# Two-layer recurrent decoder step: layer 1 planned with VectorE alone waiting for GpSimd; half-size products for the second head of layer 2, built from a copy of the normed x1 in DRAM

## The chip, the cores and the metric

The kernel runs on one core of one Trainium2 chip, as a single launch. The metric is the device time of that launch in microseconds (us); lower is better. The kernel before took 1070.28 us (median of three runs: 1069.11, 1070.28, 1070.42).

## The reference

1056 tokens (1024 of a prompt and 8 sequences of 4) with 1024 features go through two layers and a last norm, all in float32:

```python
def _lru_layer(x, ...):                 # layer 1 of the text (Hawk)
    u = _rmsnorm(x, g_norm) @ w_in      # 1024 -> 2 * 1536
    xb, gate = u[..., :W_LRU], u[..., W_LRU:]
    xc, new_buf = _causal_conv(xb, conv_w, conv_b, buf)
    h, h_last = _rg_lru(xc, w_r, b_r, w_i, b_i, lam, h0)
    return x + (h * silu(gate)) @ w_out, h_last, new_buf

def _hgrn_layer(x, ...):                # layer 2 of the text (HGRN2), 8 heads of 128
    u = _rmsnorm(x, g_norm) @ w_in      # 1024 -> 4 * 1024: q, f, v, gate
    log_g = logaddexp(log(lb), log1p(-lb) + log_sigmoid(f));  k = -expm1(log_g)
    o, S_T = _hgrn2_chunked(silu(q), k, v, log_g, S0)         # decayed linear attention, states 128 x 128
    return x + (rmsnorm(o) * o_gain * silu(gate)) @ w_out, S_T
...
y = _rmsnorm(x, final_gain)             # outputs: y of both groups of tokens, and all new states
```

## The kernel before

**Products.** Tokens lie along the free dimension, features on the 128 partitions. Every float32 product is three TensorE matmuls in a 32-bit format of shorter mantissa, summed in PSUM (`mm3`, L248, L249, L250): a rounded part `xh` or `whi` of either operand and the rest `xl` or `wlo`, as xh*whi + xl*whi + xh*wlo. The rounding is a ScalarE cast, the rest a subtraction on VectorE or GpSimd (`subtract`, L331, weights and activations alike).

**Chunks.** Layer 1 and the first part of layer 2 work on three chunks `c` of 352 tokens (`CH`). A product of 128 output features of layer 2 over all tokens is then 3 chunks x 8 blocks of input features x 3 = 72 matmuls of 352 columns.

**Heads of layer 2.** A head `h` needs four products: q, f, v and gate, items 0 to 3. Heads 0 and 1 (`HC = 2`) compute all items in full. From head 2 on, items go in pairs (0, 1) and (3, 2), and each pair is one two-by-two block product by Strassen and Winograd (`seven`): seven half-size products instead of eight, each over 264 tokens (`QT`) at a time, 2 x 4 x 3 = 24 matmuls of 264 columns. They need sums of weights (VectorE, L1441) and sums `t` of the normed x1, taken between the token halves (`HT` = 528 apart) and the feature halves. A string like "126b74b35" sets the order of the seven products, and `b` in it places a burst of the head's other work.

**The sums t.** `build` makes three of the four sets of sums, TB[2], TB[3] and TB[4], from `xh` and `xl` with seven VectorE operations of 264 columns for each of 8 pieces (j, x) (L1371), three casts on ScalarE (L1374), and three remainders on GpSimd (L331). `build1` makes the fourth set in place over the upper token half of the first four blocks of `xh` and `xl`, so only when the full products no longer read them: 8 pieces with three VectorE additions and one VectorE remainder each. Product 6 reads TB[2], products 7 and 4 TB[4] and TB[3], product 5 the fourth set.

**The bursts.** The recurrence of a head is four bursts of small work on all engines (`burst1` to `burst4`), placed between the large products; burst 4 ends with `turned(h)`: v and the weighted keys of head h go to DRAM (`vt`, `kt`) and come back with the token blocks on other partitions, each as one store of 512 KB and four loads of 128 KB. `states` (L1216, TensorE) of the next head's burst 2 reads both. The gated output of a head is stored to DRAM (`yd`, 528 KB) by `gated`.

**What sets the order.** Each layer's operations are recorded with an engine, an estimated duration, the buffers read and written, and a priority (`Flow.add`). `Flow.plan` is a list scheduler over all engines, repeated with the times of `back`; for layer 1 a random search of 3000 tries over the first 60 us follows. The order that comes out is issued as it stands, so every engine and the SP queue, which issues nearly all DMAs, work in a fixed order, and an instruction that waits holds up what stands behind it there. The planner has a model of VectorE and GpSimd getting in each other's way: a two-input VectorE operation that starts while GpSimd works is lengthened until GpSimd is done (`taken`), and a GpSimd operation that starts during such a VectorE operation is lengthened likewise (`locked`).

In the trace `sg`, `R`, `tmp`, `a` and `k` are large work buffers with changing contents, `hg` and `mm` PSUM banks, `t` the cast sums, `wraw` weights as loaded, and `si` the incoming states.

Of the kernel before, what the change touches and what calls it, by code (L numbers as in the profile page):

```python
# [42 lines left out]
NCH = 3  # L43
# [8 lines left out]
class Flow:  # L52
# [7 lines left out]

    def __init__(self, until=None, side=1.2, busy=None):


        self.until = until
        self.busy = {e: (busy or {}).get(e, 0.0) for e in self.ENGINES}
# [37 lines left out]
    def plan(self, key, stop=None):  # L103
# [11 lines left out]
        for _ in range(n):  # L115
# [101 lines left out]
def tile_trunk(ctx: ExitStack, tc: tile.TileContext, xT, prm, hc, w0, wg, wo0, w1, wo1, s_in,  # L217
# [18 lines left out]
    def pc(name, j, n=1):  # L236
        a = PRM[name][0] + j
        return P[:, a:a + n]
# [33 lines left out]

    x1a = [nc.dram_tensor(f"x1a_{m}", (128, TOK), F32, kind="Internal").ap() for m in range(KD)]
    x1d = [nc.dram_tensor(f"x1_{m}", (128, TOK), F32, kind="Internal").ap() for m in range(KD)]

# [27 lines left out]
    with ExitStack() as l0:  # L303
        pl = l0.enter_context(tc.tile_pool(name="l0", bufs=1, reuse_waits="tile"))
        fl = Flow("PE")

# [8 lines left out]

        def dma(dst, src, r=(), w=(), prio=5, kb=180, q=Q):
            fl.add("SP" if q is Q else "ACT", 0.45, lambda: q.dma_start(dst, src), r, w, prio, kb * (1.0 if r else 0.75))

# [337 lines left out]
        def out_last(src):  # L656
# [42 lines left out]
            for c in range(NCH):  # L699
# [233 lines left out]
    with ExitStack() as l1:  # L933
# [229 lines left out]
        def turned(h, row, rk, dst, key, keys):  # L1163

            d = turn[key, h % 2]
            dve(1024, lambda: V.transpose(dst, row[:, :1024].rearrange("p (n b i) -> p b n i", n=8, b=4)), rk, keys, 3, True)
            dma(d, dst, keys, ((key, "d", h % 2),), 3, 512)
            back = d.rearrange("(a i) (b m) -> b i a m", a=4, b=4)
            for b in range(4):
                dma(dst[32 * b:32 * b + 32].rearrange("p (a m) -> p a m", a=4), back[b], ((key, "d", h % 2),), (keys[b],), 3, 128)  # L1170

# [136 lines left out]
        def gated(h, s, sk):  # L1308
# [41 lines left out]
        def build(j, temps):  # L1350

            for x in range(2):
                t, tk = next(temps)
                lo, up = slice(x * QT, x * QT + QT), slice(HT + x * QT, HT + x * QT + QT)
                q, k = lo, ("x12", j, x)
                F = lambda o: o.bitcast(F32)
                chain = ((3, (xh[j + 4], up, 1), (xh[j], up, -1), (xl[j + 4], up, 1), (xl[j], up, -1)),
                         (2, (xh[j], lo, 1), (xl[j], lo, 1)), (4, (xh[j + 4], lo, 0), (xl[j + 4], lo, 1)))
                for n, *steps in chain:
                    if n == 3:  # L1360
                        (a, u, _), (b, v, _), *steps = steps
                        add(QT, t, F(a[:, u]), F(b[:, v]), ALU.subtract, (k,), tk)
                    for a, u, sign in steps:
                        if sign == 0:
                            add(QT, t, F(a[:, u]), t, ALU.subtract, (tk,), tk)
                        else:
                            add(QT, t, t, F(a[:, u]), ALU.add if sign > 0 else ALU.subtract, (tk, k), tk)
                    parted_sum(n, j, x, TB[n, 0][:, j, q], TB[n, 1][:, j, q], t, tk, G)

# [6 lines left out]

        def build1(temps):

            for j in range(4):
                for x in range(2):  # L1380
                    t, tk = next(temps)
                    lo, up = slice(x * QT, x * QT + QT), slice(HT + x * QT, HT + x * QT + QT)
                    F = lambda o: o.bitcast(F32)
                    h, l = xh[j], xl[j]
                    k = ("x12", j, x)
                    add(QT, t, F(h[:, up]), F(h[:, lo]), ALU.subtract, (k,), tk)
                    add(QT, t, t, F(l[:, up]), ALU.add, (tk, k), tk)
                    add(QT, t, t, F(l[:, lo]), ALU.subtract, (tk,), tk)
                    for i in range(2):
                        inherit(("T", 1, i, j, x), [k, *((("xh", "xl")[i], j, c) for c in (1, 2))])  # L1390
                    parted_sum(1, j, x, h[:, up], l[:, up], t, tk, V)

# [129 lines left out]
        own_gate(0)  # L1522
        spots = [(R[:, 3, i * QT:i * QT + QT], ("tmp", 2 + i)) for i in range(4)]
        small_ = [(tmp[:, i], ("tmp", i)) for i in range(2)]
        temps = cycle(small_ + spots)
        for j in range(4):
            build(j, temps)
        for h in range(HC):
            order = [item(h, i) for i in ((0, 1, 3, 2) if h else (3, 2))]
            seq_ = [(i, c) for i in range(len(order)) for c in range(NCH)]  # L1530
            if h == HC - 1:
                seq_ = seq_[:-6] + [(len(order) - 2 + i, c) for c in (2, 1, 0) for i in (0, 1)]
            ws2 = {} if h else ahead
            for n, (i, c) in enumerate(seq_):
# [3 lines left out]
                if h and n == 5:  # L1538
# [4 lines left out]
        build1(cycle(small_))  # L1543
        mm, hg = cycle(banks8[:NM7]), cycle(banks8[NM7:])
# [12 lines left out]

        for h in range(HC, H):
            seven(h, 0, 1, FQ0 if h == HC else FQ, (lambda h=h: burst3(h - 1), lambda h=h: burst4(h - 1)))
            own_gate(h)  # L1560
            seven(h, 3, 2, GV, (lambda h=h: burst1(h), lambda h=h: burst2(h)))

# [252 lines left out]
```

## Time and profile before

| | before |
|---|---|
| median of three runs | 1070.28 us |
| span of the profiled execution | 1069.7 us |
| TensorE matmuls | 1045.4 us busy, 98% |
| VectorE | 817.2 us, 76% |
| ScalarE | 574.2 us, 54% |
| GpSimd | 520.1 us, 49% |
| moved by DMA | 119.89 MB, 112 GB/s |

The profile counts an engine busy from the start of an instruction to its end. Matmuls overlap one another, so TensorE's 98% says that something is nearly always in flight; what one matmul takes is read from the distance between two starts. The profiled execution's own time is its span, with nothing of the program outside it; it lies 0.6 us under the median of the runs. Layer 1 ends near 510 us, where the first products of layer 2 take over. A clock of 1.00 means that TensorE's clock was granted in full.

### The profile page before, as it was taken

The page shows a single profiled execution, that of the slowest core. Times are in us where ns is not written, and L with a number is a line of the kernel's source. Part 1 is how long each engine was busy: PE and PEld are TensorE (multiplying, and loading weights), DVE is VectorE, ACT ScalarE, POOL GpSimd, SP SyncE. Part 2 cuts the span into 40 slices and gives each one's busy share as a digit, 9 for nine tenths or more (in the row PEclk, how much of TensorE's full clock was granted, in tenths as well). Part 3 has the DMA queues.
Part 4 walks back from the last instruction along what each step waited for, and adds up shares of the span by engine and source line. Part 5 has one row for each costly group of instructions (what it writes and reads, how often), then busy time and mean ns, then how long its engine had stood idle before and what let it go on. Part 6 is the DMA issues. An engine that isn't in the chain of part 4 may idle for free.

```text
span 1069.7 us, 26257 instructions
## 1 busy us (share of the span) xinstructions
PE 1045.4 (98%) x10220; PEld 1013.1 (95%) x10220; DVE 817.2 (76%) x1626; ACT 574.2 (54%) x1308; POOL 520.1 (49%) x601
## 2 busy tenths in 40 slices
PE   9899999999999999999999999999999999999997
PEld 9789999999999999999999998999999999999986
DVE  8999667589698788454697899787878787995436
ACT  6576745966856786433344363544545454562324
POOL 2425234345345355735567455555555554652544
PEclk9999999999999999999999999999999999999999
DMA  8201112212681387432113015242424242577204
GB/s 282 78 14 56 37 44 61 68 53 67 182 258 56 104 265 245 147 111 73 59 62 104 9 61 162 81 150 73 140 83 140 84 139 84 164 222 217 85 1 163
DMA packets 81644, 119.89 MB, mean 112 GB/s; under 512 B 10480, under 2 KB 59632, under 8 KB 81520
## 3 DMA queue, kind: packets, MB, share of 16 engines
q1 hardware_dynamic: 79216, 115.46, 34.4%
q10 hardware_dynamic: 2304, 2.77, 0.7%
q8 instruction: 80, 1.31, 0.5%
q14 instruction: 44, 0.36, 0.1%
HBM read 79.44 MB, written 33.87 MB: 106 GB/s over the span
## 4 chain that ended last, share of the span: by engine, by line
PE 85%; DVE 9%; issue 2%; DMA 1%; POOL 1%; ACT 0%; SPq 0%; ACTq 0%; POOLq 0%; DVEq 0%
PE mm L248 24%; PE mm L250 23%; PE mm L249 23%; PE hg L1216 2%; PE hg L1063 1%; PE hg L1271 1%; PE hg L575 1%; DVE sg L466 1%; PE hg L1273 1%; DVE xl L331 1%; PE hg L249 1%; PE hg L250 1%; PE hg L248 1%; DVE k L507 1%; DVE R L441 1%
## 5 line engine op out<-in xcount | busy, mean ns | idle before, releaser
L248 PE MATMUL mm<-xh,whi 128*128 128x352 f32 (+1 forms) x1143 | 358.6, 314 | 0.0
L250 PE MATMUL mm<-xh,wlo 128*128 128x352 f32 (+1 forms) x1143 | 354.8, 310 | 1.1 <-POOL wlo L331 1.1
L249 PE MATMUL mm<-xl,whi 128*128 128x352 f32 (+1 forms) x1143 | 354.3, 310 | 0.5 <-POOL xl L331 0.5
L331 POOL TENSOR_TENSOR wlo<-wraw,whi 128x256 fp32r<-128x256 f32 (+3 forms) x184 | 198.9, 1097 | 214.8 <-ACT whi L386 114.9
L249 PEld LDWEIGHTS mm<-xl,whi 128*128 128x128 f32 x1143 | 215.8, 189 | 2.2 <-POOL xl L331 0.8
L248 PEld LDWEIGHTS mm<-xh,whi 128*128 128x128 f32 x1143 | 215.5, 189 | 1.7
L250 PEld LDWEIGHTS mm<-xh,wlo 128*128 128x128 f32 x1143 | 215.6, 189 | 1.4 <-POOL wlo L331 1.4
L507 DVE SCALAR_TENSOR_TENSOR k<-xb,prm_sb,k 128x352 f32<-128x352 f32 (+2 forms) x144 | 87.0, 615 | 23.0 <-ACT k L504 19.9
L248 PE MATMUL mm<-t,whi 128*128 128x264 f32 (+1 forms) x306 | 89.6, 293 | 0.1
L249 PE MATMUL mm<-t,whi 128*128 128x264 f32 (+1 forms) x306 | 87.7, 287 | 0.0
L250 PE MATMUL mm<-t,wlo 128*128 128x264 f32 (+1 forms) x306 | 87.5, 286 | 0.0
L1504 DVE TENSOR_TENSOR k<-mm,k 128x264 f32<-128x264 f32 x144 | 60.1, 424 | 23.4 <-PE mm L250 21.7
L331 POOL TENSOR_TENSOR wlo<-R,whi 128x256 fp32r<-128x256 f32 x64 | 56.0, 895 | 28.1 <-ACT whi L1431 27.1
L590 POOL TENSOR_TENSOR k<-X 128x352 f32<-128x352 f32 x36 | 44.2, 1235 | 46.6 <-DVE R L591 32.7
L386 ACT CAST whi<-wraw 128x512 fp32r<-128x512 f32 (+2 forms) x83 | 46.3, 575 | 27.8 <-PE mm L249 12.4
L248 PEld LDWEIGHTS mm<-t,whi 128*128 128x128 f32 x306 | 57.5, 188 | 0.9 <-ACT krep L1003 0.3
L250 PEld LDWEIGHTS mm<-t,wlo 128*128 128x128 f32 x306 | 57.7, 189 | 0.0
L249 PEld LDWEIGHTS mm<-t,whi 128*128 128x128 f32 x306 | 57.6, 188 | 0.0
L1431 ACT CAST whi<-wraw 128x512 fp32r<-128x512 f32 x52 | 32.0, 618 | 41.6 <-PE mm L250 13.9
L248 PE MATMUL mm<-yh,whi 128*128 128x352 f32 x153 | 51.3, 336 | 0.0
L250 PE MATMUL mm<-yh,wlo 128*128 128x352 f32 x153 | 49.4, 323 | 0.0
L249 PE MATMUL mm<-yl,whi 128*128 128x352 f32 x153 | 49.4, 323 | 0.0
(459 smaller groups left out, 2557.9 us busy)
## 6 DMA issues: line engine op xcount, KB each, us to landing
wraw<-in_w_dram SPq DMA_DIRECT2D x90, 256.0 KB, 2.9
wraw<-in_wo_dram SPq DMA_DIRECT2D x34, 192.0 KB, 2.5
si<-in_s_in_dram SPq DMA_DIRECT2D x8, 512.0 KB, 5.5
vt<-sg SPq DMA_DIRECT2D x8, 512.0 KB, 2.9
sg<-vt SPq DMA_DIRECT2D x32, 128.0 KB, 3.0
kt<-kt SPq DMA_DIRECT2D x8, 512.0 KB, 3.0
kt<-kt SPq DMA_DIRECT2D x32, 128.0 KB, 4.3
out_ss_out_dram<-si SPq DMA_DIRECT2D x8, 512.0 KB, 2.7
```

The lines of the kernel that those rows point to most:

```text
L248: T.matmul(out, wh, xh, start=first, stop=False)
L249: T.matmul(out, wh, xl, start=False, stop=False)
L250: T.matmul(out, wl, xh, start=False, stop=last)
L331: emit = lambda: e.tensor_tensor(b, x, a.bitcast(F32), op=ALU.subtract)
L386: act(m, lambda hi=hi, raw=raw, m=m: S.copy(hi[:, :m], raw[:, :m]), rk, (hk,), prio)
L441: (pool if e is G else dve)(CH, lambda: e.tensor_tensor(a[:, :CH], a[:, :CH], sq, op=ALU.add), (sk, ak), (ak,), 2)
L466: dve(CH, lambda: V.scalar_tensor_tensor(x, x, g, bc, op0=ALU.mult, op1=ALU.mult), (xk, bk, gk), (xk,), prio)
L507: dve(u, lambda src=src, dst=dst, sh=sh, k=k: V.scalar_tensor_tensor(dst, sh(src, k), pc("cw", 12 * k + m), dst, op0=ALU.mult, op1=ALU.add ...
L590: pool(CH, lambda x=x, a=a, b=b: G.tensor_tensor(x, a.bitcast(F32), b.bitcast(F32), op=ALU.add), (ak, bk), (xk,), 3)
L1216: T.matmul(ps[w, n * 128:(n + 1) * 128], kt[:, 4 * i + n, a], vt[:, 4 * i + n], start=True, stop=True, tile_position=(0, 32 * a))
L1431: act(512, lambda: S.copy(hi, raw), (rk,), (hk,), 2)
L1504: dve(QT, lambda: V.tensor_tensor(o[0], z[0], u[0], op=ALU.add), (z[1], u[1]), (o[1],), 0)
```

## The change

It has six parts, all in the order and the layer-2 set-up; no arithmetic of a result is dropped.

1. **Layer 1's plan.** Its `Flow` is told `yields=False`: a GpSimd operation is no longer lengthened by a VectorE operation in the model. Layer 1 is planned anew with that, and its order differs from the first microseconds on.
2. **A copy of the normed x1.** After its scaling and splitting, each 128 x 352 piece of the normed x1 is also stored to DRAM (`xnd`): 24 stores of 180 KB on SP.
3. **The sums from that copy.** `build` loads four 264-column pieces of it for each (j, x) (32 loads of 132 KB, into 12 pads) and needs three additions instead of seven; the three remainders move from GpSimd to VectorE. `build1` loads two pieces (16 loads) and needs one addition and one remainder. VectorE operations: 56 to 48 in `build`, 32 to 16 in `build1`; GpSimd: 24 to 0.
4. **Head 1's items 3 and 2 by seven half-size products**, with the new order "126b743b5". Two full items, 144 matmuls of 352 columns, become 168 of 264. Head 1's bursts 1 and 2 stand within them, and the weights of the pair get combined like those of later heads.
5. **The yd store** of a head waits until the next head's `kt` is back (`kept`), and stands behind it on SP.
6. **The planner's figures** for the four loads of `turned` are raised (250 KB and 0.7 us each).

```diff
-FQ0, FQ, GV = "126b74b35", "12b675b43", "126b754b3"
+GV0, FQ, GV = "126b743b5", "12b675b43", "126b754b3"
-SPOTS, SPOTS0, SPOTS1 = (6, 9, 0, 2), (2, 5, -1, -1), (1, 5, 9, 13, 17, 20)
+SPOTS, SPOTS0, SPOTS1 = (-1, -1, 0, 2), (2, 5, -1, -1), (1, 5, 9, 13, 17, 20)
...
             if both:
                 us += max(0.0, taken - t0 - 0.085)
-                locked = t0 + us
+                locked = t0 + us if self.yields else 0.0
...
-        fl = Flow("PE")
+        fl = Flow("PE", yields=False)
...
                     scaled_parts(c, m, x, xk, bc, bk, pc("g1", m), ("P",), G if m % 4 == 3 else V, 4)
+                    dma(xnd[m][:, chunk(c)], x, (xk,), (("xnd", m, c),), 5)
...
-                dma(dst[32 * b:32 * b + 32]..., back[b], ((key, "d", h % 2),), (keys[b],), 3, 128)
+                dma(dst[32 * b:32 * b + 32]..., back[b], ((key, "d", h % 2),), (keys[b],), 3, 250, us=0.7)
...
-            if h < H - 2:
-                dma(yd[h], SG[h], ykeys(h % 2, 0, TOK), (("yd", h),), 4, 528)
+        def kept(h):
+            dma(yd[h], SG[h], (*ykeys(h % 2, 0, TOK), *KK), (("yd", h),), 4, 528)
...
                 turned(h, *brow(h, 0), kflat, "kt", KK)
+            if 0 < h < H - 1:
+                kept(h - 1)
+        def build(j, x, pads):
+            lo, up = x * QT, HT + x * QT
+            (t22, k22), (t12, k12), (t11, k11), (t21, k21) = (piece(next(pads), *o) for o in ((j + 4, up), (j, up), (j, lo), (j + 4, lo)))
+            q = slice(lo, lo + QT)
+            add(QT, t22, t22, t12, ALU.subtract, (k22, k12), k22)
+            parted_sum(3, j, x, TB[3, 0][:, j, q], TB[3, 1][:, j, q], t22, k22, V)
+            add(QT, t11, t11, t22, ALU.add, (k22, k11), k11)
+            parted_sum(2, j, x, TB[2, 0][:, j, q], TB[2, 1][:, j, q], t11, k11, V)
+            add(QT, t21, t21, t11, ALU.subtract, (k21, k11), k21)
+            parted_sum(4, j, x, TB[4, 0][:, j, q], TB[4, 1][:, j, q], t21, k21, V)
...
-            order = [item(h, i) for i in ((0, 1, 3, 2) if h else (3, 2))]
+            order = [item(h, i) for i in ((0, 1) if h else (3, 2))]
...
-        for h in range(HC, H):
-            seven(h, 0, 1, FQ0 if h == HC else FQ, (lambda h=h: burst3(h - 1), lambda h=h: burst4(h - 1)))
-            own_gate(h)
-            seven(h, 3, 2, GV, (lambda h=h: burst1(h), lambda h=h: burst2(h)))
+        for h in range(HC - 1, H):
+            if h >= HC:
+                seven(h, 0, 1, FQ, (lambda h=h: burst3(h - 1), lambda h=h: burst4(h - 1)))
+                own_gate(h)
+            seven(h, 3, 2, GV if h >= HC else GV0, (lambda h=h: burst1(h), lambda h=h: burst2(h)))
```

Lines move by one to five: L248 to L250 are L249 to L251 after the change, L317 is L319, L331 is L333, L1063 is L1066.

Three places show what that does to the order. First the SP queue at `turned(1)`, in head 2 of layer 2, before the change:

```order
L317 DMA vt<-sg 128x1024
L317 DMA wraw<-in_w_dram 128x512
L317 DMA out_ss_out_dram<-si 128x1024
L317 DMA sg<-vt 32x4x256 x4
L317 DMA kt<-kt 128x1024
L317 DMA R<-in_w_dram 128x512
L317 DMA wraw<-in_w_dram 128x512
L317 DMA yd<-sg 128x1056
L317 DMA si<-in_s_in_dram 128x1024
L317 DMA wraw<-in_w_dram 128x512
L317 DMA kt<-kt 32x4x256 x4
```

The same place of the SP queue after it:

```order
L319 DMA vt<-sg 128x1024
L319 DMA sg<-vt 32x4x256 x4
L319 DMA kt<-kt 128x1024
L319 DMA out_ss_out_dram<-si 128x1024
L319 DMA wraw<-in_w_dram 128x512
L319 DMA kt<-kt 32x4x256 x4
L319 DMA si<-in_s_in_dram 128x1024
L319 DMA wraw<-in_w_dram 128x512
L319 DMA R<-in_w_dram 128x512 x2
L319 DMA yd<-sg 128x1056
```

Between the store of `kt` and its four loads back stood two weight blocks, a further block of weights, `yd` and `si`; now there stand the store of the outgoing state and one block of weights, and `yd` and `si` follow the loads.

Second TensorE in head 1, at burst 1 (the rows of L1063 and L1176 before, of L1066 and L1179 after). Before, it lies between full products:

```order
L248 MATMUL mm<-xh,whi 128x352
L249 MATMUL mm<-xl,whi 128x352
L250 MATMUL mm<-xh,wlo 128x352
L1063 MATMUL hg<-R,a 32x64 x32
L1083 MATMUL hg<-R,a 32x64
L1176 MATMUL hg<-ident,krep 96x128
L1176 MATMUL hg<-ident,vrep 96x128
L248 MATMUL mm<-xh,whi 128x352
```

After, product 6 (which reads TB[2], here t_5227 and t_5228) stands ahead of it, and product 7 behind it:

```order
L249 MATMUL mm<-t_5227,whi 128x264
L250 MATMUL mm<-t_5228,whi 128x264
L251 MATMUL mm<-t_5227,wlo 128x264
L1066 MATMUL hg<-R,a 32x64 x32
L1086 MATMUL mm<-R,a 32x64
L1179 MATMUL mm<-ident,krep 96x128
L1179 MATMUL mm<-ident,vrep 96x128
L249 MATMUL mm<-t_5229,whi 128x264
```

TensorE's first need of a sum thus moves ahead of head 1's burst 1; before, it came in head 2.

Third VectorE in the start of layer 1, around the first remainder of chunk 1 (`xl<-sg,xh`). Before:

```order
L537 SCALAR_TENSOR_TENSOR sg<-k,sg 128x352 x2
L466 SCALAR_TENSOR_TENSOR sg<-sg,g_166,hg 128x352 x2
L456 TENSOR_TENSOR k<-ident,nr_132 128x256
L466 SCALAR_TENSOR_TENSOR sg<-sg,g_166,hg 128x352 x2
L507 SCALAR_TENSOR_TENSOR k<-xb_135,prm_sb,k 128x352
L331 TENSOR_TENSOR xl<-sg,xh 128x352
```

After:

```order
L468 SCALAR_TENSOR_TENSOR sg<-sg,g_166,hg 128x352 x2
L455 TENSOR_SCALAR nr_132<-hg 96x1
L468 SCALAR_TENSOR_TENSOR sg<-sg,g_166,hg 128x352
L490 TENSOR_TENSOR xb_134<-mm,R 128x352
L468 SCALAR_TENSOR_TENSOR sg<-sg,g_166,hg 128x352
L333 TENSOR_TENSOR xl<-sg,xh 128x352
```

That first remainder stood at row 93 of VectorE's order and stands at row 110 now, behind work on the convolution's blocks (`k`, `xb`).

More of the change, by code (lines that the diff above doesn't have):

```diff
@@ L59, with __init__ @@
     ends = []
-    def __init__(self, until=None, side=1.2, busy=None):
+    def __init__(self, until=None, side=1.2, busy=None, yields=True):
         self.until = until
+        self.yields = yields
         self.busy = {e: (busy or {}).get(e, 0.0) for e in self.ENGINES}
@@ L273, in tile_trunk @@
     x1a = [nc.dram_tensor(f"x1a_{m}", (128, TOK), F32, kind="Internal").ap() for m in range(KD)]
+    xnd = [nc.dram_tensor(f"xn_{m}", (128, TOK), F32, kind="Internal").ap() for m in range(KD)]
     x1d = [nc.dram_tensor(f"x1_{m}", (128, TOK), F32, kind="Internal").ap() for m in range(KD)]
@@ L1347, in burst4, with piece @@
                 turned(h, *brow(h, 0), kflat, "kt", KK)
[L1350 to L1368, printed above, removed]
+            if 0 < h < H - 1:
+                kept(h - 1)
+        def piece(pad, k, a):
+            t, tk = pad
+            dma(t, xnd[k][:, a:a + QT], (), (tk,), 4, 132)
+            return pad
+        def build(j, x, pads):
[8 more added lines that the diff above has]
+            parted_sum(4, j, x, TB[4, 0][:, j, q], TB[4, 1][:, j, q], t21, k21, V)
         def add(n, o, a, b, op, r, w, prio=5):
@@ L1375, in parted_sum, with build1 @@
             subtract(e, QT, lo, t, hi, (tk, ("T", n, 0, j, x)), (("T", n, 1, j, x),), prio)
[L1377 to L1381, printed above, removed]
+        def build1(pads):
+            for x in range(2):
+                for j in range(4):
                     lo, up = slice(x * QT, x * QT + QT), slice(HT + x * QT, HT + x * QT + QT)
[L1383 to L1388, printed above, removed]
+                    (t, tk), (u, uk) = piece(next(pads), j, HT + x * QT), piece(next(pads), j, x * QT)
+                    add(QT, t, t, u, ALU.subtract, (tk, uk), tk)
                     for i in range(2):
-                        inherit(("T", 1, i, j, x), [k, *((("xh", "xl")[i], j, c) for c in (1, 2))])
-                    parted_sum(1, j, x, h[:, up], l[:, up], t, tk, V)
+                        inherit(("T", 1, i, j, x), [((("xh", "xl")[i], j, c)) for c in (1, 2)])
+                    parted_sum(1, j, x, xh[j][:, up], xl[j][:, up], t, tk, V)
         def operand(p, j, x):
@@ L1542, in tile_trunk @@
                         b(h if j < 2 else h - 1)
-        build1(cycle(small_))
+        own_gate(HC - 1)
+        homes = [(VT[:, i * QT:i * QT + QT], ("pad", "VT", i)) for i in range(4)]
+        for i, (_, k) in enumerate(homes):
+            inherit(k, [("VT", c) for c in range(NCH)])
+        build1(cycle(homes + [(tmp[:, i], ("tmp", i)) for i in range(2)]))
+        for i, (_, k) in enumerate(homes):
+            inherit(("VT", i), [k])
         mm, hg = cycle(banks8[:NM7]), cycle(banks8[NM7:])
```

29 lines of the change are left out of this document (16 added, 13 removed).

## The prediction

> **What bounds the kernel now.** I read the page's first part, then the busy time by stages, the groups of waits of TensorE, the chain of waits around the longest of them, and timelines for the pitch of matmuls.
>
> ```profile
> PE 1045.4 (98%) x10220; PEld 1013.1 (95%) x10220; DVE 817.2 (76%) x1626; ACT 574.2 (54%) x1308; POOL 520.1 (49%) x601
> ```
>
> TensorE is the bound. By stages (start:end, length, busy time of PE, PEld, DVE, ACT, POOL, then the granted clock):
>
> ```profile
> core 0: us, PE busy (x) PEld busy (x) DVE busy (x) ACT busy (x) POOL busy (x), PEclk, DMA share, GB/s
> ...
> 12.00:92.00 80.00, 71.20 (x413) 66.72 (x412) 77.20 (x189) 48.86 (x101) 28.77 (x37) 0.96 0.28 90
> 92.00:510.00 418.00, 418.00 (x2566) 411.84 (x2566) 299.63 (x498) 258.67 (x504) 191.98 (x212) 1.00 0.38 116
> 510.00:530.00 20.00, 19.54 (x121) 19.24 (x120) 15.54 (x27) 8.20 (x18) 14.24 (x13) 1.00 0.15 47
> 530.00:600.00 70.00, 68.18 (x982) 66.08 (x984) 57.54 (x108) 29.07 (x71) 42.01 (x43) 1.00 0.23 75
> 600.00:640.00 40.00, 39.55 (x493) 37.92 (x483) 37.03 (x79) 21.93 (x63) 22.11 (x26) 1.00 0.11 38
> 640.00:930.00 290.00, 285.43 (x4314) 275.24 (x4314) 237.66 (x518) 147.04 (x390) 157.27 (x193) 0.99 0.37 117
> ```
>
> Three limits stand here. From 12 to 92 us VectorE is the bound (77.20 of 80) and TensorE loses 8.8 us. From 92 to 510 TensorE has no gap, so no order can gain there. From 530 on it loses little: 1.82 us up to 600, 0.45 up to 640, 4.57 up to 930. Their names (engine, what was waited for, total, times, longest):
>
> ```profile
> PE hg L284 <- DVE R L441: 2.7, 2, 1.9
> PE hg L1216 <- DMA kt<-kt: 2.4, 1, 2.4
> PE hg L461 <- DVE k L459: 1.9, 2, 1.4
> PE hg L1216 <- issue: 1.8, 2, 1.1
> ...
> PE mm L250 <- POOL wlo L331: 1.1, 1, 1.1
> ...
> PE hg L1117 <- DVE R L1045: 0.7, 1, 0.7
> ...
> PE hg L1225 <- issue: 0.5, 1, 0.5
> ```
>
> L284 and L461 belong to the start; the one wait for `kt` is the longest of all. So the change can win by fewer columns, by that wait, by the small ones of 530 to 640, and in the first 92 us.
>
> **Columns.** The pitch from timelines (start, duration, line):
>
> ```profile
> 505.70 0.32 PE L249 MATMUL mm<-xl,whi 128*128 128x352 f32 x1
> ...
> 507.48 0.33 PE L248 MATMUL mm<-xh,whi 128*128 128x352 f32 x1
> ```
>
> ```profile
> 669.76 0.28 PE L250 MATMUL mm<-xh,wlo 128*128 128x264 f32 x1
> ...
> 671.47 0.28 PE L249 MATMUL mm<-xl,whi 128*128 128x264 f32 x1
> ```
>
> Eleven steps in 1.78 us are 0.162 us, fourteen in 1.71 us are 0.122 us. Head 1 loses 144 matmuls of 352 columns and gets 168 of 264: 144 x 0.161 = 23.2 us against 168 x 0.122 = 20.5 us, a gain of **2.7 us**. TensorE has no idle time there to swallow it, so it counts in full.
>
> **The wait for kt.** The chain of waits at burst 2 of head 1 and of head 2 (start, length, what):
>
> ```profile
> 598.77 1.91 PE hg L1216 x64
> ```
>
> ```profile
> 653.55 7.66 DMA kt<-kt
> 661.21 0.35 issue
> 661.57 3.58 PE hg L1216 x64
> ```
>
> The last load back of `kt` took 7.66 us to land, TensorE waited 2.4 us, and the same 64 matmuls then took 3.58 us instead of 1.91. The clock says why (the 6.6 us before, and those 3.6 us):
>
> ```profile
> 655.00:661.60 6.60, 4.21 (x158) 3.99 (x158) 6.40 (x14) 2.15 (x5) 2.98 (x5) 1.00 0.59 137
> 661.60:665.20 3.60, 3.60 (x73) 3.60 (x77) 1.65 (x6) 0.62 (x1) 2.27 (x3) 0.53 0.00 0
> ```
>
> Granted clock 0.53 after the wait: 1.6 us more. The wait costs 4.0 us in all. On SP:
>
> ```profile
> 647.14 0.38 SPq L317 DMA_DIRECT2D kt<-kt  x1
> ...
> 648.99 0.40 SPq L317 DMA_DIRECT2D yd<-sg  x1
> 649.45 0.47 SPq L317 DMA_DIRECT2D si<-in_s_in_dram  x1
> ...
> 651.48 2.54 SPq L317 DMA_DIRECT2D kt<-kt  x4
> ```
>
> The page's DMA rows give the usual landing:
>
> ```profile
> kt<-kt SPq DMA_DIRECT2D x8, 512.0 KB, 3.0
> kt<-kt SPq DMA_DIRECT2D x32, 128.0 KB, 4.3
> ```
>
> The store landed near 650.1, but the loads went out from 651.48, behind `yd`, `si` (1.04 MB together) and three blocks of weights, and landed 3.4 us later than the usual 4.3. In the new order one block of weights and the outgoing state stand between, and `yd` and `si` come behind. The loads could start near 650.2 and land by 654 to 658; TensorE, 2.7 us earlier, wants them at 661.57 - 2.4 - 2.7 = 656.5. Later heads keep the old order and do not wait, since there is more time between the transposing of `kt` and its use:
>
> ```profile
> L1166 DVE STREAM_TRANSPOSE kt<-sg x2: 1234/1235/1236, 644.5 to 694.9; 128x1024 f32<-128x1024 f32 x2
> ```
>
> ```profile
> 718.08 0.86 PE L1216 MATMUL hg<-sg,kt 128*32 128x128 f32 x23
> ```
>
> 23.2 us there, 14.7 us in head 1 without the wait (644.5 to 659.2). VectorE was late in head 1 because `build1` ran until 635; that work is halved. Bounds: nothing to -4.0, or +1 if `yd`, now later, frees its buffer late. I take **-4.0**, since order and VectorE's load both move the right way. One rule bears on the 1.6 us in it. The Trainium skill, "TensorE: Matmul & The Clock Gate" (Part 1: The HAM clock gate), has the clock halved after at least one idle window of about 3.4 us; the wait here was 2.4 us. Read strictly, that would cut the tie between this wait and the slow clock, and the sum would lose 1.6 us of its gain. The trace has the two side by side, so the row decides.
>
> **The sums.** `build` can no longer start from `xh` and `xl`; it needs the copies. The last scaling of chunk 2 and the cost of one 264-column operation:
>
> ```profile
> 517.50 0.57 DVE L466 SCALAR_TENSOR_TENSOR sg<-sg,prm_sb,hg 128x352 f32<-128x352 f32 x1
> ```
>
> ```profile
> L1371 DVE TENSOR_TENSOR tmp<-tmp,xl x32: 418/434/981, 518.7 to 631.8; 128x264 f32<-128x264 f32 x32
> ```
>
> The nearest transfer, a load of 176 KB (last column: us to landing):
>
> ```profile
> sg<-x1b SPq DMA_DIRECT2D x21, 176.0 KB, 3.1
> ```
>
> From 518.1, a store and a load of some 3 us each, with the DMA share of 0.15 there leaving room: first sums at 524 to 525, where they began at 516. On VectorE `build` falls from 56 to 48 operations, on GpSimd 24 remainders go:
>
> ```profile
> L331 POOL TENSOR_TENSOR t<-tmp,t x12: 748/948/1222, 523.1 to 596.4; 128x264 fp32r<-128x264 f32 x12
> ```
>
> 24 x 0.93 = 22 us of GpSimd against some 7 us for head 1's additional weights. In before the sums were done at 596.4, since VectorE's next sum also waited for those remainders. After it, 48 operations of 0.43 to 0.62 are 21 to 30 us of VectorE. With the rest of its order laid out at the durations of these rows, the last TB[2] comes at 560 to 570, TB[4] near 573 (estimates from the order and the rows). Need: head 1's order is unchanged up to this row of TensorE,
>
> ```profile
> 566.48 0.69 PE L1148 MATMUL hg<-R,sg 128*64 128x64 f32 x16
> ```
>
> then 72 x 0.161 and 48 x 0.122, so product 6 at 567.2 + 17.5 = 584.6. Slack of 12 us or more; covered by full products, cost nothing. The weights' sums end near 572 to 581: slack 4 at the least. The fourth set is the narrowest: 16 operations instead of 32, ready near 599.5 by the same laying-out, wanted by product 5 at 584.6 + 2.9 + 1.5 + 8.8 + 4.9 = 602.7 (product 6, burst 1, products 7, 4, 3, burst 2). Slack 3 us.
>
> With the pair's weights new, the 1.1 us for `wlo` has no place any more, while L1117 and L1225 stay. Bounds for 530 to 640: -2.3 (all its idle time) to no gain; I take **-0.7**. For new small waits (weights behind piece loads on SP, combines ahead of the casts) I put **+1.0**, about the wait for `wlo`; bounds 0 and +3.
>
> **The start.** Only here and at the same bound as before, VectorE, can the new plan act. The clock shows what a patchy start costs:
>
> ```profile
> 40.00:44.00 4.00, 3.44 (x13) 3.32 (x13) 4.00 (x12) 3.04 (x7) 2.95 (x4) 0.57 0.43 140
> ...
> 57.00:61.00 4.00, 3.47 (x12) 3.47 (x13) 4.00 (x8) 3.54 (x9) 1.56 (x3) 0.57 0.04 11
> ```
>
> TensorE is fed in full once all of chunk 1 is normed and split, near 61 us. VectorE's order after the change, laid out at the same operations' durations, splits chunk 1's last piece at 51.1 against 50.0 and scales it at 51.7 against 51.1, its first piece 3.7 us later. No work goes away. I take **+0.6**; bounds -2 (the first sums of chunk 2 no longer ahead of chunk 0's products) and +4 (one more slow window of 1.7 us and 2 us of waiting).
>
> The 24 stores and 48 loads add 10.6 MB to 119.89 MB, and some 72 issues of 0.35 us to SP, beside work; nothing else waits on them. The raised figures of `turned` move only the plan.
>
> **Sum:** -2.7 - 4.0 - 0.7 + 1.0 + 0.6 = -5.8 us on the profiled span of 1069.7 gives 1063.9. The span lies 0.6 below the median of the runs, so I forecast **1064.5 us**. 0.2%, 2.1 us, is about what a measurement of this kernel can tell from none: faster is below 1068.1, slower above 1072.4.
>
> **Rivals.**
> - *The wait for kt stays or another takes its place* (chance 0.20). For it: the landing of 7.66 us might come of the weights that still go out there, and the four loads wait for the store alone. Against: 1 MB less ahead of them. -5.8 + 4.0 = -1.8: 1068.5.
> - *All layer-2 waits of the first heads go and the start gains* (0.15): -2.7 - 4.0 - 2.3 - 1.0 = -10: 1060.3. For it: GpSimd has 15 us less to do there. Against: L1117 and L1225 are not touched.
> - *The new plan of layer 1 errs* (0.10). It plans as though GpSimd never waits. The remainders above, 748 ns at the shortest and 948 in the median, say that it does; results due from GpSimd (the last remainders of chunk 1) come late, a slow window follows: +4 instead of +0.6, 1067.9. The Trainium skill, "SBUF — State Buffer" (Who interferes with whom), says the same: a two-input VectorE operation and a GpSimd operation that reads SBUF block each other, whoever issues second waiting for the whole of the other. By that rule alone the plan before was the truer one.
> - *Head 1's fourth set comes too late* (0.13), the other side. If its operations and the eight remainders run at the slow end of their row (981 instead of 434 ns: 16 x 0.55 = 8.8 us more, and 9 us of lateness from `build` besides), product 5 waits with all later work of TensorE behind it, and the clock halves as at 661 (+1.6). It decides from a readiness of 609 on, 6.3 us late: 1064.5 + 6.3 + 1.6 = 1072.4 and more. For it: VectorE is 37.03 of 40 busy from 600 to 640. Against: GpSimd, which makes the slow end, has less to do.
> - The forecast itself has 0.42, from 1062.5 to 1067.
>
> Faster: 0.40 of the forecast's 0.42, 0.09 of the first rival, 0.15, 0.05 of the third: 0.69. Slower 0.13. Same 0.18. The range leaves out the slow rival and the lower part of the fast one, 0.19 together: 1060 to 1071.
>
> **What would show it.** Right: the wait of L1216 for `kt` gone and the clock 1.00 through head 2's burst 2; 264-column matmuls at 0.122 us from near 579 on; the sums from 524 to about 573; full TensorE between 92 and 510. Wrong: a wait of a matmul for `t` or `xl` (from L1374 or L333) near 585 or 603; a third window of slow clock before 92; or a wait for `kt` in any head, with its loads landing later than 5 us.

## The result: slower, 1077.51 us against 1070.35

The changed kernel took 1077.51 us (median of 4 runs, 1076.63 to 1078.81), the kernel before 1070.35 in the same comparison: a ratio of 1.0068, 95% interval [1.0051, 1.0086], so some 7 us slower. 1064.5 was forecast, with 1071.0 as the upper end. The profiled execution spans 1075.7 us. Its time was 1077.48: 1.7 to 1.9 us lie outside the span, in every execution listed since. The profiled execution of the kernel before, with a span of 1069.7, thus belongs to a time near 1071.5 and lies about 1 us over its median, not 0.6 under it.

The first part of the page after, and the stages as above (start:end, length, busy PE, PEld, DVE, ACT, POOL, granted clock):

```profile
PE 1047.1 (97%) x10244; PEld 1015.1 (94%) x10244; DVE 810.7 (75%) x1620; ACT 575.4 (53%) x1311; POOL 501.2 (47%) x587
```

```profile
12.00:92.00 80.00, 69.07 (x377) 66.20 (x376) 74.54 (x178) 44.84 (x95) 27.55 (x33) 0.89 0.27 87
92.00:510.00 418.00, 416.85 (x2540) 409.26 (x2540) 301.19 (x501) 259.14 (x507) 190.70 (x209) 1.00 0.40 123
510.00:530.00 20.00, 20.00 (x127) 19.79 (x126) 9.68 (x23) 8.05 (x15) 9.44 (x13) 1.00 0.28 95
530.00:600.00 70.00, 67.01 (x831) 65.39 (x830) 52.32 (x103) 31.92 (x75) 29.57 (x32) 1.00 0.54 166
600.00:640.00 40.00, 38.74 (x648) 36.80 (x646) 36.40 (x81) 18.61 (x55) 22.32 (x28) 1.00 0.24 76
640.00:930.00 290.00, 287.72 (x4292) 278.03 (x4289) 241.16 (x515) 151.00 (x397) 155.56 (x192) 1.00 0.33 110
```

From 12 to 92 us the granted clock is 0.89 instead of 0.96, and VectorE, the bound there, has less done (74.54 us instead of 77.20). TensorE's waits:

```profile
PE hg L286 <- DVE xb L443: 3.1, 1, 3.1
PE mm L250 <- DVE xl L333: 2.9, 2, 2.7
PE mm L249 <- ACT k L538: 2.9, 1, 2.9
PE hg L1066 <- DVE sg L1048: 2.3, 2, 1.8
...
PE mm L249 <- DVE attns L1073: 1.4, 1, 1.4
```

Three waits of about 3 us each stand in the start, where the kernel before had none longer than 1.9 in its profile; the wait for `kt` is gone, and two waits of layer 2 are new (L1066 in head 0, `attns` in head 7).

Where the time went is read from work that both kernels do in the same place. The sum of squares of the last chunk of x1, at the end of layer 1, before and after:

```profile
504.93 0.67 PE L284 MATMUL hg<-ones,xb 128*128 128x1 f32 x6
```

```profile
513.78 0.67 PE L286 MATMUL hg<-ones,xb 128*128 128x1 f32 x6
```

Layer 1 lost 8.85 us; all the rest, to the end of the span, won 2.85 (561.9 instead of 564.8). By 100 us, counted by the recorded 352-column matmuls (the 400th begins at 103.6 instead of 97.4), some 6.2 of the 8.85 were lost; the other 2.6 went between 150 and 505 us.

### The profile page after: what moved, and what is told of

It reads as the page before. It is cut to its first block, busy times and chain, and to the rows that moved or that the text cites. A ratio compares the mean times of both kernels' runs of the same rounds, so it can differ in the third digit from the quotient of the medians.

```text
span 1075.7 us, 26457 instructions
## 1 busy us (share of the span) xinstructions
PE 1047.1 (97%) x10244; PEld 1015.1 (94%) x10244; DVE 810.7 (75%) x1620; ACT 575.4 (53%) x1311; POOL 501.2 (47%) x587
## 4 chain that ended last, share of the span: by engine, by line
PE 82%; DVE 11%; issue 3%; ACT 1%; POOL 1%; DMA 1%; SPq 1%; POOLq 0%; DVEq 0%; ACTq 0%
PE mm L249 23%; PE mm L250 23%; PE mm L251 23%; DVE k L509 2%; PE hg L1066 2%; PE hg L1274 1%; PE hg L577 1%; PE hg L1276 1%; PE hg L249 1%; PE hg L250 1%; PE hg L251 1%; DVE xl L333 1%; PE hg L1219 1%; DVE sg L468 1%; PE mm L1219 1%
## 5 line engine op out<-in xcount | busy, mean ns | idle before, releaser
L249 PE MATMUL mm<-xh,whi 128*128 128x352 f32 (+1 forms) x1127 | 351.7, 312 | 0.0
L250 PE MATMUL mm<-xl,whi 128*128 128x352 f32 (+1 forms) x1127 | 348.0, 309 | 0.2 <-DVE xl L876 0.2
L251 PE MATMUL mm<-xh,wlo 128*128 128x352 f32 (+1 forms) x1127 | 348.0, 309 | 0.0
L333 POOL TENSOR_TENSOR wlo<-wraw,whi 128x256 fp32r<-128x256 f32 (+3 forms) x188 | 201.9, 1090 | 242.8 <-ACT whi L388 121.5
L250 PEld LDWEIGHTS mm<-xl,whi 128*128 128x128 f32 x1127 | 212.5, 189 | 2.2 <-DVE xl L876 0.7
L249 PEld LDWEIGHTS mm<-xh,whi 128*128 128x128 f32 x1127 | 212.1, 188 | 1.8
L251 PEld LDWEIGHTS mm<-xh,wlo 128*128 128x128 f32 x1127 | 212.3, 188 | 0.2 <-POOL wlo L333 0.2
L249 PE MATMUL mm<-t,whi 128*128 128x264 f32 (+1 forms) x330 | 96.5, 293 | 1.4 <-DVE attns L1073 1.4
L250 PE MATMUL mm<-t,whi 128*128 128x264 f32 (+1 forms) x330 | 94.5, 286 | 0.0
L251 PE MATMUL mm<-t,wlo 128*128 128x264 f32 (+1 forms) x330 | 94.3, 286 | 0.0
L1504 DVE TENSOR_TENSOR k<-mm,k 128x264 f32<-128x264 f32 x154 | 64.4, 425 | 21.1 <-PE mm L251 19.8
L333 POOL TENSOR_TENSOR wlo<-R,whi 128x256 fp32r<-128x256 f32 x70 | 59.7, 874 | 29.6 <-ACT whi L1431 27.7
L249 PEld LDWEIGHTS mm<-t,whi 128*128 128x128 f32 x330 | 62.1, 188 | 2.2 <-ACT krep L1006 1.6
L251 PEld LDWEIGHTS mm<-t,wlo 128*128 128x128 f32 x330 | 62.2, 188 | 0.0
L250 PEld LDWEIGHTS mm<-t,whi 128*128 128x128 f32 x330 | 62.1, 188 | 0.0
L249 PE MATMUL mm<-yh,whi 128*128 128x352 f32 x153 | 52.2, 341 | 0.0
L250 PE MATMUL mm<-yl,whi 128*128 128x352 f32 x153 | 49.4, 323 | 0.0
L251 PE MATMUL mm<-yh,wlo 128*128 128x352 f32 x153 | 49.4, 323 | 0.0
```

The lines of the kernel that those rows point to most:

```text
L249: T.matmul(out, wh, xh, start=first, stop=False)
L250: T.matmul(out, wh, xl, start=False, stop=False)
L251: T.matmul(out, wl, xh, start=False, stop=last)
L333: emit = lambda: e.tensor_tensor(b, x, a.bitcast(F32), op=ALU.subtract)
L1504: dve(QT, lambda: V.tensor_tensor(o[0], z[0], u[0], op=ALU.add), (z[1], u[1]), (o[1],), 0)
```

## The experiments

Twelve runs, in three groups. "Layer 1" below is the start of that last sum of squares in the run's profile, "the rest" what the span has after it.

### Is it the new plan of layer 1?

**Everything but the plan.** The edit to the changed kernel:

```diff
-        fl = Flow("PE", yields=False)
+        fl = Flow("PE")
```

> The changed kernel with layer 1 planned as before (GpSimd waits in the model again); everything of layer 2 stays changed. Layer 1's order on VectorE is then that of the kernel before. Theory A (the new plan of layer 1 is what costs: TensorE stands 8.85 us later than before at the last norm of x1, 513.78 against 504.93, and the end only 6.0 us later): the end comes 8 to 9 us earlier than with the whole change, 1067 to 1069.5, and the start of layer 1 shows two windows of slow clock, not six. Rival B (the 24 stores of the normed x1, or a start that turns out differently in any run): 1075 to 1078.

Measured: 1069.22 us, ratio to the kernel before 0.9988 [0.9978, 0.9997]. Layer 1 504.66, the rest 562.5. As theory A had it for the time: with the old plan the 24 stores of x1 cost nothing in layer 1. It also showed that the rest of the change is worth 1.3 us, not the 6.4 of the forecast.

**The plan alone.** The kernel before with the `yields` argument, and `Flow("PE", yields=False)` for layer 1.

> The kernel before with only layer 1's plan changed (VectorE alone waits in the model). Theory A: 8 to 9 us slower than before, 1078 to 1080, lost by 100 us for the most part (about 6 us) with four more windows of slow clock. Rival B: as before, 1069 to 1072.

Measured: 1079.48 us, 1.0087 [1.0073, 1.01]; layer 1 513.65. The plan by itself costs 9.3 us, as theory A had it. The two parts, +9.3 and -1.3, make 8.0, within the interval of the whole (5.5 to 9.2). The four more windows of slow clock did not come, though. Here is the stretch from 12 to 92 us of this run:

```profile
12.00:92.00 80.00, 68.22 (x390) 64.53 (x389) 75.26 (x180) 45.38 (x97) 27.92 (x34) 0.94 0.27 88
```

The granted clock is 0.94, against 0.89 in the changed kernel and 0.96 before, and still layer 1 ends within 0.2 us of the changed kernel's. How often the clock is low differs between executions of one order, and most of the plan's loss does not hang on it.

### Why does the plan cost, and is it the model or the search?

TensorE in the start of the changed kernel (start, duration; in brackets the idle time before and what ended it):

```profile
25.96 1.33 PE L286 MATMUL hg<-ones,xb 128*128 128x1 f32 x6 [3.10 <-DVE xb L443]
...
40.72 0.63 PE L249 MATMUL mm<-xh,yh 128*128 128x352 f32 x1 [2.91 <-ACT k L538]
41.15 0.49 PE L250 MATMUL mm<-xl,yh 128*128 128x352 f32 x1
41.44 0.49 PE L251 MATMUL mm<-xh,yl 128*128 128x352 f32 x1
...
56.81 0.66 PE L250 MATMUL mm<-xl,X 128*128 128x352 f32 x1 [2.73 <-DVE xl L333]
```

After each wait the pitch is 0.29 us (41.15 to 41.44) instead of 0.16: half the clock. That this can hurt is seen on VectorE, at 47 us:

```profile
DVE xb L490 <- PE mm L251: 2.4, 1, 2.4
```

VectorE, which sets the pace of the start, stood still for 2.4 us since the product that it waited for ran at half speed (in the run with the plan alone it stood still for 1.2 us). Before, it waited for nothing between 36 and 54 us.

**Work in the gaps.** In the changed kernel, matmuls of a constant block of ones into a bank that is about to be overwritten (they leave no result) at the three places:

```diff
+SUMS, BCS, WARMS, PRODS = {0: 12}, {}, {45: 12}, {6: 11}
...
+        def filler(o, n):
+            for _ in range(n):
+                T.matmul(o[:, :128], ones, ones, start=True, stop=True)
```

> The changed kernel with idle work for TensorE in three places of the start: 12 small matmuls of ones ahead of the first sums of squares (2.8 us, where it idles 3.1 us at 22.9), 12 at 37.8 (idle 2.9 us) and 11 ahead of the first product of chunk 1 (idle 2.7 us at 54). Theory S (most of the start's loss is the slow clock that follows idle stretches of about 3 us: the pitch of 352 columns is 0.29 us from 26 to 32.6, 40.7 to 46.1 and 56.8 to 59.9): those windows go, layer 1 ends 3 to 6 us earlier, 1071.5 to 1074.5. Rival V (VectorE sets the start; a faster TensorE only waits longer): 1076 to 1079.

Measured: 1077.6 us, 1.0054 [1.0039, 1.0069] of before, which the changed kernel's 1.0068 [1.0051, 1.0086] overlaps. The stretch from 40 to 50 us, in the changed kernel and with fillers:

```profile
40.00:50.00 10.00, 9.28 (x45) 9.31 (x46) 7.52 (x19) 3.49 (x8) 3.26 (x5) 0.68 0.30 97
```

```profile
40.00:50.00 10.00, 9.06 (x59) 8.88 (x60) 9.88 (x25) 4.68 (x11) 3.74 (x6) 1.00 0.32 103
```

The clock is full and VectorE has no gap. By 100 us this brought back 3.1 of the 6.2 us. But layer 1 ended at 512.70, only 1.1 earlier: in this execution a matmul of layer 1's gates (`hg<-X,gh` in the trace) then waited 1.3 us for ScalarE near 403 us, among others. The rest took 563.8 us, 1.9 longer than in the changed kernel's profile, and why is not known. So the slow clock is up to half of what this order had lost at 100 us, and the end shows next to nothing of the half regained. With the clock full, TensorE is 1.2 us behind the kernel before at 80 us, much what the prediction had laid out for VectorE, and loses 1.9 more between 80 and 100 us, where the matmuls of the gates wait for VectorE and ScalarE. Rival V holds for the time, though not for its reason, since TensorE did get ahead. Of theory S the windows went as it said, and the time did not.

**Other seeds of the search.** `Random(1)` became `Random(2)` in the kernel with the new plan alone, and in the kernel before; then `Random(3)` with the new plan.

> The kernel before with layer 1 planned by the new model, and another seed of the planner's random search. Theory M (a plan that takes GpSimd as never waiting is bad whatever the search finds): 1076 to 1082, near the 1079.5 of the first seed. Rival L (the search's luck): anywhere else, 1069 to 1075.

> The kernel before, as it is, with the other seed. Theory M: within 2 us of before, 1069 to 1073. Rival L: several us off, 1074 to 1080.

> The kernel before with layer 1 planned by the new model and a third seed. Theory M' (the new model costs by itself: in both seeds the matmuls of the gates wait between 255 and 312 us, and the last norm starts 5.5 and 8.7 us later): the last norm 5 to 9 us later than the 504.9 of before, waits for R or X of the gates near 260 and 310. Rival L (luck of the search alone): the last norm within 2 us of 504.9 in one of three seeds.

| layer 1's model | seed | ratio to before | layer 1 ends | the rest |
|---|---|---|---|---|
| GpSimd never waits | 1 | 1.0087 [1.0073, 1.01] | 513.65 | 563.3 |
| GpSimd never waits | 2 | 1.0012 [1.0002, 1.0022] | 510.43 | 561.5 |
| GpSimd never waits | 3 | 1.0042 [1.0028, 1.0056] | 511.87 | 561.8 |
| both wait (before) | 1 | 1 | 504.93 | 564.8 |
| both wait | 2 | 1.0003 [0.9992, 1.0013] | 506.23 | 562.3 |

Theory M's times were missed by the second seed, 1072.85 us, which fits rival L; the old model's second seed took 1071.39 us, as theory M had it. But layer 1 ends 5.5, 6.9 and 8.7 us late with the new model and 1.3 with the old model's second seed. The model costs 4 to 9 us of layer 1, and the search moves that by some 3 us. The rest differs by up to 3 us between plans that have the same layer 2, which hides some of it in the times. The third seed came out as theory M' had it, and none of the three ends layer 1 within the 2 us of rival L.

What do the new model's orders share? Each has idle stretches of TensorE of about 3 us in the start (3.1, 3.8 and 2.7 in the run of seed 1, 3.8 with seed 2, 3.2 and 2.9 with seed 3). But the old plan can have one too: 2.8 with its second seed, and 2.8 and 2.9 near 85 us in two other executions of its first. The loss after the start says more. Counted by the 352-column matmuls, the runs stand behind the kernel before by:

| layer 1's model, seed | at 80 us | at 100 us | at the end of layer 1 |
|---|---|---|---|
| GpSimd never waits, 1 | 3.3 | 5.4 | 8.7 |
| GpSimd never waits, 2 | 0.1 | 2.6 | 5.5 |
| GpSimd never waits, 3 | 1.1 | 2.6 | 6.9 |
| both wait, 2 | 0.4 | 0.1 | 1.3 |

The random search covers only the first 60 us. Past 80 us all three seeds lose 5.4 to 5.8 us, the old model's second seed 0.9, and with all three, matmuls of the gates wait at the same places near 260, 270 and 310 us. One of them waits for ScalarE's `R` near 310 us in all six profiles with the new model's orders, for 0.5 to 0.8 us, and in none of the seven with the old model's and no fillers. From 150 to 505 us, in the changed kernel, with seed 2 and with seed 3:

```profile
PE hg L249 <- ACT R L573: 0.6, 1, 0.6
```

```profile
PE hg L249 <- ACT R L572: 0.8, 1, 0.8
```

```profile
PE hg L249 <- ACT R L572: 0.7, 1, 0.7
```

Three seeds and two are few, and which placements of the new model make the gates' inputs late was not isolated.

### Which part of layer 2's change gives, and which takes?

**The late yd store and the figures for turned taken back**, in the changed kernel with its new plan, and then on top of the old plan:

```diff
-        def kept(h):
...
+            if h < H - 2:
+                dma(yd[h], SG[h], ykeys(h % 2, 0, TOK), (("yd", h),), 4, 528)
...
-                dma(..., (keys[b],), 3, 250, us=0.7)
+                dma(..., (keys[b],), 3, 128)
```

> The changed kernel with the yd store and the planner's figures for the loads of turned as before; the yd store and si stand ahead of the loads of kt again. Theory (the order on SP made the wait for kt): the wait of L1219 for kt in head 2 comes back with its slow window, 2 to 4 us slower than the whole change, 1079.5 to 1081.5. Rival (the wait went since build1 is shorter and VectorE is ahead): no wait for kt, 1076 to 1078.5.

> The changed kernel with layer 1 planned as before and the yd store and the figures for turned as before: what is left are the copy of x1, the sums from it, and head 1's seven products. The profile of the run with the early yd store put layer 2 at 553.5 us from the last norm to the end, against 556.3 with the late one and the old plan. Theory (the late yd store gives nothing once build1 is short, and the plan around build is better without it): 1066 to 1068. Rival (that difference is one execution's): as with the old plan alone, 1068.5 to 1070.

Measured: 1076.22 us with the new plan, 1.0057 [1.0045, 1.007], the rest 559.8; with the old plan 1067.37, **0.9961 [0.9948, 0.9974]**, the rest 559.9. The wait for `kt` did not return in either, though `yd` and `si` stood ahead of its loads again: with this layer 2 the order on SP does not make it, as the first rival had it. The second run came out as its theory had it. What went is the wait of burst 2 in head 0 (TensorE, waits from 530 to 640 us), first in the changed kernel, then with the old plan and the early yd:

```profile
PE hg L1066 <- DVE sg L1048: 2.3, 2, 1.8
PE hg L1219 <- issue: 1.2, 1, 1.2
PE hg L1120 <- DVE R L1048: 0.7, 1, 0.7
```

```profile
PE hg L1219 <- issue: 1.1, 1, 1.1
PE hg L1120 <- DVE a L1048: 0.5, 1, 0.5
PE hg L1066 <- DVE sg L1048: 0.2, 1, 0.2
```

VectorE just before that wait, in the changed kernel:

```profile
558.96 1.35 DVE L1376 TENSOR_TENSOR sg<-sg 128x264 f32<-128x264 f32 x3
560.23 0.43 DVE L1376 TENSOR_TENSOR a<-a 128x264 f32<-128x264 f32 x1
560.57 0.70 DVE L1048 TENSOR_TENSOR sg<-a,sg 128x528 f32<-128x528 f32 x1
```

Four of the sums (L1376) stand ahead of the operation of the burst (L1048) that TensorE waits for. With the early yd and the old plan that operation runs at 543.00, 7.7 us before its use.

**The late yd and the raised figures on the kernel before.**

> The kernel before with only the later yd store and the planner's figures for the loads of turned. Theory (order on SP): the wait for kt at 661 us goes, and with it its slow window: 3 to 4 us faster, 1066 to 1067.5. Rival (VectorE late by build1): kt itself is late, the wait stays in part, 1069 to 1071.

Measured: 1069.14 us, 0.9988 [0.9977, 0.9999]: 1.3 us and not 3 to 4; the rest took 560.9. There is no wait for `kt` in its profile, so the wait went as the theory had it, but the time is the rival's. But neither is there one with the kernel before's layer 2 in two of the four other executions (0 with the new plan's seeds 1 and 2, 0.4 us with the old plan's seed 2, 1.2 with the new plan's seed 3). The 2.4 us were the longest wait of five executions.

**The early yd with the new figures.**

> As the kernel of the last job with the old plan and the early yd, but with the raised figures for the loads of turned (250 KB, 0.7 us). Tells which of the two, the later yd or the figures, brings the wait of L1066 for VectorE's sg in head 0 (1.8 to 2.0 us with both, 0.2 without both). If the yd store itself: ratio 0.995 to 0.997 and no such wait. If any other plan of that stretch: 0.998 to 0.999 and the wait.

Measured: 1069.72 us, 0.9989 [0.998, 0.9998], the rest 561.6, and the wait is back:

```profile
PE hg L1066 <- DVE sg L1048: 1.9, 1, 1.9
```

Not the store but the raised figures bring it: with them the planner puts the sums ahead of the burst. They cost 1.7 us by the profiles (561.6 against 559.9) and some 3 by the times (0.9989 against 0.9961). The late store with the old figures was not run.

**The sums' remainders on GpSimd again**, on the kernel with the old plan and the early yd: `V` became `G` in the three calls of `parted_sum` in `build`.

> The kernel of the last job with the old plan and the early yd, but with the 24 remainders of the sums on GpSimd again. Theory (they are hidden either way: TB[2] is wanted only near 584 us): as without, ratio 0.995 to 0.997. Rival (VectorE waits for GpSimd as before the change, and the sums come late): a wait for t near 585, 0.998 or more.

Measured: 1067.24 us, 0.9972 [0.9961, 0.9982], the rest 559.8, no wait for `t`. Where the 24 remainders run makes no difference that shows, as the theory had it.

**Fillers on the best version.** The old plan and the early yd, with fillers ahead of the sums of squares and the broadcasts (`SUMS = {0: 5, 1: 8, 2: 3}`, `BCS = {0: 6, 1: 2}`).

> The changed kernel with layer 1 planned as before, yd and the figures for turned as before (1067.4 us in the last job, 0.9961 of before), and small matmuls of ones in the idle stretches of the start: 5, 8 and 3 ahead of the three sums of squares, 6 and 2 ahead of the first two broadcasts. The clock is granted in full in the start. Theory S (a slow window of 3.4 us costs up to 1.7 us, and the plan of before runs into one or two of them): 1 to 3 us faster than without, ratio to before 0.993 to 0.995. Rival V (VectorE sets the start): no change, 0.9955 to 0.9965, or slower by fillers that run past the data, 0.997.

Measured: 1068.93 us, 0.9985 [0.9975, 0.9995]. The clock was full up to 50 us, and by 100 us TensorE stood where it stood without (its 400th recorded 352-column matmul at 97.3 us, 97.5 without, 97.4 in the kernel before). With the old plan VectorE sets the start, and the slow windows that the fillers took away had cost nothing there. So far rival V is right. But the launch is slower than without the fillers (0.9985 against 0.9961 and 0.9972), more than even rival V allowed. In the profile layer 1 ends 0.8 us later and the rest takes 561.5 us, 1.6 more, with a wait of 2.7 us near 935 us (the longest of this row) that the runs without fillers do not have:

```profile
PE mm L1236 <- issue: 3.3, 2, 2.7
```

The other run with fillers has one of 1.75 us on that line in head 7. Whether the fillers make these waits is not shown.

## Why the prediction was wrong, point by point

**The start, +0.6: the step that failed.** The sum laid out VectorE's new order as if VectorE never waited, read its price off the end of chunk 1's splits, 1.1 us later, and had no term for anything of layer 1 behind it. Layer 1 ended 8.85 us later by the profile, and the plan alone cost 9.3 us by the times. In the place of that step the runs showed three losses. First, the order makes TensorE idle for three stretches of about 3 us in the start; the clock is halved behind each, and VectorE then waits for TensorE. With the clock kept full, 3.1 of the 6.2 us lost by 100 us came back, and 1.1 at the end of layer 1. Second, 1.4 to 2.6 us are lost between 80 and 100 us with each of the three seeds, where the gates' matmuls wait. Third, 2.6 us and more went later in layer 1. What in the new order makes those inputs late stays open.

The upper bound of +4 allowed for one more slow window. The granted clock of 0.89 instead of 0.96 over 80 us is 5.6 us of clock more, or three such windows, and the sign of being wrong, a third window before 92 us, was there. But the same order at a clock of 0.94 ended layer 1 at the same point. The rival "the new plan of layer 1 errs" had the right part of the change, at a chance of 0.10, and its price of +4 was less than half. Its way to it, results of GpSimd that come late, is not what the waits show: the three long ones are for VectorE's `xb` and `xl` and ScalarE's `k`.

**"TensorE has no gap from 92 to 510, so no order can gain there."** None can gain; one can lose. 2.6 us went there, in part for gates' matmuls that waited (0.8 us named between 150 and 505 us), where the old plan has no gap. No term stood for it.

**The wait for kt, -4.0.** It did go, but its length was that of the one profiled execution, which was also about 1 us above the median. The reading behind it was off as well: the store of `kt` took 4.3 us to land there, not the 3.0 of the page's median, so it landed at 651.4 and not near 650.1, and the loads that went out at 651.48 had waited for it, and not for `yd` and `si`. By itself the late yd, with the raised figures, was worth 1.3 us (0.1 to 2.5 by its interval). The order on SP, on which the step rested, made no difference with the new layer 2: there, with the early yd, the store of `kt` goes out 129.0 us after the last norm starts, where it was 142.2 before. That VectorE's shorter `build1` does this fits, but it was not tried by itself. A wait that only some executions have moves the median by a part of its length.

**530 to 640 us, -0.7, and the raised figures, costed at nothing.** TensorE's idle time there did not fall but rose, from 2.27 to 4.25 us. The raised figures moved the plan, and that was 1.8 us of a new wait in head 0. The plan of that stretch was in the order and was not read against burst 2.

**Small new waits, +1.0.** Besides that one there is 1.4 for `attns` in head 7, which is in seven of the eight profiles with the new layer 2 and, with at most 0.2 us, in those with the old one. What brings it was not tried.

**The columns, -2.7: right.** The same point of the diagonal blocks in heads 0 and 1, before and after:

```profile
566.09 0.46 PE L1141 MATMUL mm<-R,a 128*32 128x32 f32 x32
...
631.55 0.46 PE L1141 MATMUL hg<-R,a 128*32 128x32 f32 x32
```

```profile
576.71 0.46 PE L1144 MATMUL mm<-R,a 128*32 128x32 f32 x32
...
639.00 0.46 PE L1144 MATMUL hg<-R,a 128*32 128x32 f32 x32
```

65.46 us became 62.29. In between, 216 matmuls of 352 columns and 120 of 264 became 72 and 288. From start to start, without the wait for `wlo` among them, they took 50.1 us before and 47.3 after, so 2.8 of the 3.2 us are columns.

**The sums' slack: right.** No matmul of the changed kernel waits for `t`, and none waits for the fourth set near product 5, so its 3 us of slack were enough. The rival on the other side did not happen; the slow outcome came from another place.

**Adding up.** The forecast was 13.0 us too low. Layer 1 makes 8.25 of that (8.85 instead of 0.6) and the rest 3.55 (-2.85 instead of -6.4). The last 1.2 is the base: the sum put 0.6 us between span and time, where 1.8 lie.

With everything of the change, the rest takes 561.9 us in the changed kernel, 562.5 with the old plan and 563.8 with fillers, against 561.5 to 564.8 in five executions with the layer 2 of before. With the early yd and the old figures it takes 559.8 to 559.9 in three profiles and 561.5 in the one with fillers. By the times the copy of x1, the sums and the half-size products are worth 3 to 4 us (0.9972 and 0.9961), of which 2.8 are columns; the raised figures take 2 to 3 of that, and the plan of layer 1 costs 9.

The best version measured has the half-size products with layer 1's plan, the yd store and the figures as before: 0.9961 [0.9948, 0.9974], and 0.9972 [0.9961, 0.9982] with the remainders on GpSimd.

## What to carry to other kernels

Where two engines feed each other in a ramp, laying out one engine's new order by its durations shows only what that engine does when nobody keeps it waiting; the order of both has to be walked together. A new order also has to be read to its end, since a stretch without gaps can get some: here more than half of what the new orders lost came after 80 us. A wait or a slow window seen in one profiled execution is worth its full length only if other executions have it too: compare the profiled span with the spans of the other runs first. In a planned kernel a change of cost figures is a change of order, and has its own price.

## What the runs showed of the hardware that was not expected

Idle stretches of 3.1, 2.9 and 2.7 us were each followed by half the clock, for 6.6, 5.4 and 3.1 us at a pitch of 0.29 us; fillers in them kept the clock at 1.00. The Trainium skill, "TensorE: Matmul & The Clock Gate" (Part 1: The HAM clock gate), names an idle window of about 3.4 us; here shorter idle stretches did it.

The length of the idle stretch alone does not decide it. The same matmul of a gate near 85 us waited 2.86 us with the late yd alone and 2.81 us with the old plan and the early yd. From 88.9 to 92.3 us the granted clock was 0.50 in the first and 1.00 in the second. What decides is not shown.

Whether a slow window costs depends on who sets the pace. With the old plan the windows fell near 25, 30, 40 or 57 us in five executions, and at 100 us TensorE stood at the same point within 0.4 us. In a sixth, the late yd alone, one fell at 88.9 us, where TensorE had work waiting; it then stood 1.4 us or more behind the others, and layer 1 ended at 506.4 us instead of 504.7 to 505.0.
